# A hybrid decoder layer on one Trainium2 core: convolution taps taken from PSUM, the decays of a token block made in one go, and the decay product moved to GpSimd

## The chip, the core and the metric

The kernel runs as one program on one core of a Trainium2 chip. The metric is the device time of a run in microseconds; lower is better. The core has five engines with in-order queues of their own: TensorE (PE, with its weight loads shown as PEld), VectorE (DVE), ScalarE (ACT), GpSimd (POOL) and SyncE (SP), which issues all DMAs of this kernel. An engine that comes to an instruction whose inputs or buffers are not ready waits there, and everything behind it in its queue waits too.

## What is computed

One layer (DEPTH is 1) of a decoder on 2048 tokens of width 1024, all in float32: a mixer with three head groups, a SwiGLU block of width 2816, a gated per-layer embedding, and a final norm. What matters here are the mixer's group A (Mamba-2 SSD) and the depthwise convolutions of width 4, cut from the reference:

```
def _causal_dwconv(x, w, b):              # y[t] = b + sum_j w[j] * x[t - 3 + j], each channel alone
...
xbc = jax.nn.silu(_causal_dwconv(xbc, ssd_conv_w, ssd_conv_b))      # 896 channels: x 384, B 256, C 256
...
acs = jnp.cumsum(ac, axis=2)                                         # inside a chunk of 128 tokens
seg = acs[:, :, :, None, :] - acs[:, :, None, :, :]
lmat = jnp.exp(jnp.where(causal[None, None, :, :, None], seg, -jnp.inf))
scores = jnp.einsum("bclhn,bcshn->bclsh", cc, bc) * lmat             # (C B) times the decays
y_diag = jnp.einsum("bclsh,bcshp->bclhp", scores, xc)
decay_s = jnp.exp(acs[:, :, -1:, :] - acs)
states = jnp.einsum("bclhn,bclh,bclhp->bchpn", bc, decay_s, xc)
chunk_decay = jnp.exp(acs[:, :, -1, :])
...
xl = _causal_dwconv(lru_x, lru_conv_w, lru_conv_b)                   # group B, 256 channels
```

Group A has 6 heads of 64 in two groups with a state of 128; there are 16 chunks.

## The kernel before

Features lie on the 128 partitions, tokens along the free axis, in four blocks (`tb`) of 512 tokens. There are three stages. `phase1` norms the input, makes group B with its two convolution blocks per token block (`lru`), the values and gates, and q. `phase1b` makes group A: for each token block the normed input is loaded again and split, then come 7 calls of `conv` (one for each 128 channels of x, B and C), 4 calls of `ssd_chunk`, the z gate, k, and a norm whose result goes to DRAM. From the second block on, the attention of the first query block is interleaved with its matmuls (`Side`, `attention`), and in the last block the output projection of the first token block. `phase3` does the rest of the layer, with the other query blocks' attention interleaved.

Every large projection is `mm3`: input and weight are split in a rounded part and a rest, and three products of them are summed, so 24 matmuls of 128x512 per 128 output channels. Its weights come by `weight`: a DMA into `wst` (2 buffers), a rounding copy on ACT (L179), and the rest by a subtraction on POOL (L180), into `w` (3 buffers). The result lies in a PSUM bank `mm`, of which there are three. Single banks `xa` to `xe` serve the rest.

In `conv`, ACT copies the projection from `mm` to SBUF behind three columns of the block before (`raw`, one buffer, L435; L434 and L438 move the halo on DVE), then makes the last tap with the bias (L437), which is the last reader of the bank; the other three taps are multiply-adds on DVE (L440) of `raw` and the accumulator. For the 28 calls in `phase1b` a tanh (L444) and a product (L445) follow.

In `ssd_chunk`, bank `xb` holds in turn C B for two groups and B transposed (`pgb`), the diagonal product (`psd`, L509) and the transposed output (`py`); the row sums `ab` come by a DMA that broadcasts 6 rows over the partitions (L457, two buffers); L471 to L476 make the small decays; L479 makes, head by head, the differences with the mask added; ACT takes the exponential (L480); L488 multiplies it with C B from PSUM; `psd` takes it as the stationary operand.

The program is traced in the order of the code, with some parts at a higher priority, and a planner with a timing model of the engines then sets the order on each engine.

Of the kernel before, what the change touches and what calls it, by code (L numbers as in the profile page):

```python
# [13 lines left out]
ACT = mybir.ActivationFunctionType  # L14
ALU = mybir.AluOpType
# [4 lines left out]
P = 128  # L20
# [44 lines left out]
class Trunk:  # L65
# [317 lines left out]
    def phase1b(self, ctx):  # L383

        nc, tc, a = self.nc, self.tc, self.a
        pool = lambda name, bufs, **kw: ctx.enter_context(tc.tile_pool(name=name, bufs=bufs, **kw))
        one = pool("m2one", 1)
        two = pool("m2two", 2)
        self.load_mpar(one)
        hcw = self.t(one, [P, 35], "hcw")  # L390
        nc.vector.tensor_scalar(hcw, self.pc("scw", 0, 35), 0.5, None, op0=ALU.mult)
        self.neg = self.t(one, [P, P], "neg")
        nc.sync.dma_start(self.neg, a["cst"][:, 2])
        halo = self.t(one, [P, 7, 3], "halo")
        nc.gpsimd.memset(halo, 0.0)
        state = None
        for tb in range(NTB):
            if tb == 1:
                self.att_setup()
                self.side.start(self.attention(0, one, ("xc", "xd"), "xe"))  # L400
            u = []
            for k in range(KD):
                u.append(self.parts(k, self.load(self.du[tb, k]), nc.gpsimd))
            dtc = self.t(two, [P, 2, NCH, 6], "dtc")
            nc.sync.dma_start(dtc, self.ddt[tb])
            xbc = []
            for b in range(7):
                xbc.append(self.conv(a["w_xbc"][b], u, halo[:, b], hcw[:, 4 * b:4 * b + 4], hcw[:, 28 + b:29 + b],
                                     two, (two, f"xbc{b}", 1) if tb % 2 and b else (self.hp, "h", None), True))
            ys = [self.t(two, [P, TB], f"ys{j}", bufs=1) for j in range(3)]  # L410
            if tb == NTB - 1:

                yx = self.load_y(0)
            for c in range(NCH):
                state = self.ssd_chunk(tb, c, xbc, dtc, state, ys, two)
            if tb == NTB - 1:
                h = [self.mix(0, c, yx) for c in range(KD)]
                self.first = h, self.norm_split(h, "g2", eng=nc.vector, tag="xd")
            for b in range(3):
                ps = self.mm3(self.weight(a["w_z"][b], KD), u, 3)  # L420
                z = self.t(two, [P, TB], "t0")
                nc.scalar.activation(z, ps, ACT.Tanh, scale=0.5)
                nc.vector.scalar_tensor_tensor(z, z, 1.0, ps, op0=ALU.add, op1=ALU.mult)
                nc.vector.scalar_tensor_tensor(ys[b], ys[b], 0.5, z, op0=ALU.mult, op1=ALU.mult)
            for b in range(3):
                self.qk("w_k", b, tb, u, two)
            self.norm_store(ys, 384, 0, tb, "xa")

    def conv(self, wsrc, u, halo, cw, cb, two, dst, silu):

        nc = self.nc
        ps = self.mm3(self.weight(wsrc, KD), u, 3)
        raw = self.t(two, [P, TB + 3], "raw", bufs=1)
        nc.vector.tensor_copy(raw[:, 0:3], halo)  # L434
        nc.scalar.activation(raw[:, 3:], ps, ACT.Copy)  # L435
        acc = self.t(dst[0], [P, TB], dst[1], bufs=dst[2])
        nc.scalar.activation(acc, ps, ACT.Identity, bias=cb, scale=cw[:, 3:4])  # L437
        nc.vector.tensor_copy(halo, raw[:, TB:TB + 3])  # L438
        for j in range(3):
            nc.vector.scalar_tensor_tensor(acc, raw[:, j:j + TB], cw[:, j:j + 1], acc, op0=ALU.mult, op1=ALU.add)  # L440
        if not silu:
            return acc
        th = self.t(two, [P, TB], "t0")
        nc.scalar.activation(th, acc, ACT.Tanh)  # L444
        nc.vector.scalar_tensor_tensor(acc, th, 1.0, acc, op0=ALU.add, op1=ALU.mult)  # L445
        return acc

    def ssd_chunk(self, tb, c, xbc, small, state, ys, two):
        nc = self.nc
        cs = slice(c * P, (c + 1) * P)  # L450
        xs, bm, cm = xbc[0:3], xbc[3:5], xbc[5:7]
        first = state is None
        dt = small[:, 0, c]
        acol = small[:, 1, c]

        ab = self.t(two, [P, 6, P], "ab")
        nc.sync.dma_start(ab, self.drow[tb, c * 12 + 6:c * 12 + 12].partition_broadcast(P))  # L457

        ptr = self.ps("xa", (P, 3, P))
        for j in range(3):  # L460
            nc.tensor.transpose(ptr[:, j], xs[j][:, cs], self.ident)
        pgb = self.ps("xb", (P, 4, P))
        for g in range(2):
            nc.tensor.matmul(pgb[:, g], lhsT=bm[g][:, cs], rhs=cm[g][:, cs], start=True, stop=True)
        for g in range(2):
            nc.tensor.transpose(pgb[:, 2 + g], bm[g][:, cs], self.ident)
        bt = self.t(two, [P, 2, P], "bt", bufs=1)
        nc.scalar.activation(bt, pgb[:, 2:4], ACT.Copy)

        ex = self.t(two, [P, 3, 6], "ex")  # L470
        nc.vector.tensor_copy(ex[:, 0], ab[:, :, P - 1])  # L471
        nc.vector.tensor_tensor(ex[:, 1], ab[:, :, P - 1], acol, op=ALU.subtract)
        nc.vector.tensor_copy(ex[:, 2], acol)
        nc.scalar.activation(ex, ex, ACT.Exp)
        dec = self.t(two, [P, 6], "dec")
        nc.vector.tensor_tensor(dec, ex[:, 1], dt, op=ALU.mult)  # L476
        seg = self.t(two, [P, 6, P], "seg", bufs=1)
        for h in range(6):
            nc.vector.scalar_tensor_tensor(seg[:, h], ab[:, h], acol[:, h:h + 1], self.neg, op0=ALU.subtract, op1=ALU.add)  # L479
        nc.scalar.activation(seg, seg, ACT.Exp)  # L480

        px = ptr.rearrange("p j (i e) -> p (j i) e", i=2)
        xc = self.t(two, [P, 6, 64], "xc", bufs=1)
        nc.vector.tensor_tensor(xc, px, dt.unsqueeze(2).to_broadcast([P, 6, 64]), op=ALU.mult)
        xd = self.t(two, [P, 6, 64], "xd", bufs=1)
        nc.vector.tensor_tensor(xd, px, dec.unsqueeze(2).to_broadcast([P, 6, 64]), op=ALU.mult)
        for g in range(2):
            nc.vector.tensor_tensor(seg[:, 3 * g:3 * g + 3], seg[:, 3 * g:3 * g + 3],  # L488
                                    pgb[:, g].unsqueeze(1).to_broadcast([P, 3, P]), op=ALU.mult)

        yt = self.t(two, [P, 6, 64], "yt", bufs=1)
        if not first:
            pso = self.ps("xa", (P, 6, 64))
            for g in range(2):
                nc.tensor.matmul(pso[:, 3 * g:3 * g + 3], lhsT=cm[g][:, cs], rhs=state[:, 3 * g:3 * g + 3], start=True, stop=True)
            nc.vector.tensor_tensor(yt, pso, ex[:, 2].unsqueeze(2).to_broadcast([P, 6, 64]), op=ALU.mult)

        pst = self.ps("xa", (P, 6, 64))
        for g in range(2):
            nc.tensor.matmul(pst[:, 3 * g:3 * g + 3], lhsT=bt[:, g], rhs=xd[:, 3 * g:3 * g + 3], start=True, stop=True)  # L500
        ns = self.t(two, [P, 6, 64], "state")
        if first:
# [297 lines left out]

# [10 lines left out]
```

## Time and profile before

| | |
|---|---|
| median of 3 runs | 2930.53 us (2925.57 to 2932.34) |
| the profiled execution | 2928.33 us, of which span 2926.6 us |
| PE busy | 2812.5 us (96%) |
| DVE busy | 1751.9 us (60%) |
| ACT busy | 1175.7 us (40%) |
| POOL busy | 1213.2 us (41%) |
| mean granted clock of PE | 0.984 |

The span runs from the first to the last instruction; what lies around it is 1.7 us. Busy time of an engine includes time in which a started instruction is held up. `phase1` takes the first 325 us or so, `phase1b` the time to about 780 us, `phase3` the rest; neighbouring stages overlap a little.

### The profile page before, as it was taken

To read this page: it belongs to the slowest core of one execution; us is meant where nothing else is said; L and a number is where in the kernel's file an instruction comes from. 1 tells how busy PE (TensorE), PEld (TensorE's weight loads), DVE (VectorE), ACT (ScalarE), POOL (GpSimd) and SP (SyncE) were. 2 spreads that over 40 slices of the span, in tenths; PEclk is the share of its full clock that TensorE was granted. 3 is DMA by queue.
4 is the path that set the end of the run, shared out by engine and by line. 5 is a ranking of instruction groups with operands and counts; after the bars stand their busy time and mean duration, and the time that the engine had idled before them with its cause. 6 is when DMAs were issued, how large, how long until landed. Compare 5 with 4: busy or idle time off the path is not lost.

```text
span 2926.6 us, 35034 instructions
## 1 busy us (share of the span) xinstructions
PE 2812.5 (96%) x12981; PEld 2317.3 (79%) x12981; DVE 1751.9 (60%) x3001; ACT 1175.7 (40%) x1751; POOL 1213.2 (41%) x635
## 2 busy tenths in 40 slices
PE   6998999998999999999999999999999999999997
PEld 5777777777888888887888888788888887888885
DVE  7888768988754543637655446464665464523246
ACT  5555434444333332434444334344444343322233
POOL 5544445432443434443333334443333344444442
PEclk9999999998999999999999999999999999999998
DMA  5544544452354343434343334243443233332231
GB/s 181 172 164 159 162 142 141 132 162 80 136 157 131 119 122 104 142 123 133 118 147 104 127 105 146 100 146 115 133 122 114 91 130 108 116 97 92 100 100 65
DMA packets 156221, 368.60 MB, mean 126 GB/s; under 512 B 17644, under 2 KB 49036, under 8 KB 154508
## 3 DMA queue, kind: packets, MB, share of 16 engines
q1 hardware_dynamic: 156050, 366.36, 38.6%
q8 instruction: 103, 1.69, 0.2%
q14 instruction: 68, 0.56, 0.1%
HBM read 322.01 MB, written 44.29 MB: 125 GB/s over the span
## 4 chain that ended last, share of the span: by engine, by line
PE 72%; DVE 3%; issue 1%; DMA 1%; ACT 1%; POOL 0%; POOLq 0%; DVEq 0%; ACTq 0%
PE mm L191 20%; PE mm L192 20%; PE mm L190 20%; PE xd L609 2%; PE xd L608 2%; PE xa L603 1%; DMA ld<-dy 1%; PE xe L603 1%; PE xb L603 1%; PE xc L603 1%; PE xa L572 0%; PE xa L573 0%; DVE th L719 0%; DVE u L168 0%; PE xb L573 0%
## 5 line engine op out<-in xcount | busy, mean ns | idle before, releaser
L180 POOL TENSOR_TENSOR w<-wst,w 128x1024 fp32r<-128x1024 f32 (+1 forms) x424 | 1031.8, 2435 | 1365.6 <-ACT w L179 1300.5
L190 PE MATMUL mm<-u,w 128*128 128x512 f32 x3264 | 1295.9, 399 | 16.5 <-ACT u L200 8.9
L191 PE MATMUL mm<-u,w 128*128 128x512 f32 x3264 | 1289.6, 396 | 13.5 <-DVE u L201 13.5
L192 PE MATMUL mm<-u,w 128*128 128x512 f32 x3264 | 1289.9, 396 | 0.5 <-POOL w L180 0.5
L190 PEld LDWEIGHTS mm<-u,w 128*128 128x128 f32 x3264 | 619.1, 190 | 144.3 <-ACT u L200 10.8
L191 PEld LDWEIGHTS mm<-u,w 128*128 128x128 f32 x3264 | 619.0, 190 | 140.9 <-DVE u L201 17.9
L192 PEld LDWEIGHTS mm<-u,w 128*128 128x128 f32 x3264 | 618.6, 190 | 128.3 <-POOL w L180 0.9
L179 ACT ACTIVATE w<-wst 128x1024 fp32r<-128x1024 f32 (+1 forms) x424 | 440.5, 1040 | 525.1 <-PE mm L192 383.1
L685 DVE SCALAR_TENSOR_TENSOR u<-th,u 128x512 fp32r<-128x512 f32 x88 | 190.6, 2166 | 62.8 <-ACT u L684 62.7
L584 ACT ACTIVATE lg<-lg,m 128x128 f32<-128x128 f32 (+7 forms) x96 | 115.5, 1203 | 155.9 <-DVE m L582 150.9
L161 DVE TENSOR_TENSOR ssq<-ssq,sq 128x512 f32<-128x512 f32 x111 | 134.6, 1212 | 58.0 <-ACT sq L157 55.8
L682 DVE TENSOR_TENSOR th<-th,mm 128x512 f32<-128x512 f32 x88 | 60.4, 686 | 168.0 <-PE mm L192 167.3
L691 DVE TENSOR_TENSOR h<-h,mm 128x512 f32<-128x512 f32 x96 | 65.6, 686 | 127.1 <-PE mm L192 126.7
L680 ACT ACTIVATE th<-mm 128x512 f32<-128x512 f32 x88 | 52.6, 597 | 214.0 <-PE mm L192 213.7
L681 DVE SCALAR_TENSOR_TENSOR th<-th,mm 128x512 f32<-128x512 f32 x88 | 60.3, 685 | 113.1 <-ACT th L680 112.9
L564 POOL TENSOR_TENSOR cd<-cum,maskT 128x128 f32<-128x128 f32 x96 | 47.9, 499 | 182.3 <-DVE mx L577 92.3
L719 DVE SCALAR_TENSOR_TENSOR th<-th,lg 128x512 f32<-128x512 f32 x32 | 31.0, 968 | 111.5 <-ACT th L718 111.4
L587 DVE TENSOR_SCALAR lg<-lg,r 128x128 f32<-128x128 f32 (+7 forms) x96 | 93.6, 975 | 2.6
L609 PE MATMUL xd<-ph,vc 128*128 128x512 f32 x216 | 83.5, 390 | 0.0
L608 PE MATMUL xd<-ph,vc 128*128 128x512 f32 x216 | 80.8, 374 | 0.0
L607 DVE TENSOR_TENSOR ph<-xc,ph 128x512 fp32r<-128x512 f32 (+1 forms) x66 | 36.7, 556 | 48.4 <-ACT ph L606 48.4
L139 POOL TENSOR_TENSOR rr<-rv,mhalf 128x4 f32<-128x4 f32 x28 | 29.1, 1041 | 88.1 <-DVE rv L137 75.3
(293 smaller groups left out, 3212.2 us busy)
## 6 DMA issues: line engine op xcount, KB each, us to landing
wst<-in_w_gate SPq DMA_DIRECT2D x88, 512.0 KB, 3.5
wst<-in_w_up SPq DMA_DIRECT2D x88, 512.0 KB, 3.5
wst<-in_w_down SPq DMA_DIRECT2D x64, 448.0 KB, 3.3
wst<-in_w_out SPq DMA_DIRECT2D x32, 512.0 KB, 3.5
wst<-in_w_down SPq DMA_DIRECT2D x32, 512.0 KB, 3.5
wst<-in_w_pg SPq DMA_DIRECT2D x32, 512.0 KB, 3.5
vc<-dv SPq DMA_DIRECT2D x60, 256.0 KB, 3.8
wst<-in_w_xbc SPq DMA_DIRECT2D x28, 512.0 KB, 4.5
```

What stands on the lines that cost most here:

```text
L161: (eng or nc.gpsimd).tensor_tensor(acc, acc, s, op=ALU.add)
L179: nc.scalar.activation(w[:, 0], st, ACT.Copy)
L180: nc.gpsimd.tensor_tensor(w[:, 1], st, w[:, 0].bitcast(F32), op=ALU.subtract)
L190: nc.tensor.matmul(ps, lhsT=w[:, 0, k], rhs=x[:, 0], start=k == 0, stop=False)
L191: nc.tensor.matmul(ps, lhsT=w[:, 0, k], rhs=x[:, 1], start=False, stop=False)
L192: nc.tensor.matmul(ps, lhsT=w[:, 1, k], rhs=x[:, 0], start=False, stop=k == n - 1)
L584: nc.scalar.activation(lg, lg, ACT.Exp, bias=m, scale=1.0, accum_out=l)
L587: nc.vector.tensor_scalar(lg, lg, r, None, op0=ALU.mult)
L603: nc.tensor.transpose(pt[:, qi * P:(qi + 1) * P], probs[qi][:, kt * P:(kt + 1) * P], self.ident)
L608: nc.tensor.matmul(po[:, sl], lhsT=vc[:, kt], rhs=ph[:, 0, sl], start=kt == 0, stop=False)
L609: nc.tensor.matmul(po[:, sl], lhsT=vc[:, kt], rhs=ph[:, 1, sl], start=False, stop=kt == nkt - 1)
L685: nc.vector.scalar_tensor_tensor(hh[:, 1], th, 0.5, hh[:, 0].bitcast(F32), op0=ALU.mult, op1=ALU.subtract)
```

## The change

- `conv`: `raw` goes. The three taps read the bank `mm`, shifted by 1 to 3 columns in the accumulator. A copy of the last three columns (`end`, ACT) goes to POOL, where five small instructions make the next block's three halo sums; DVE adds the sums of the block before to the accumulator's first three columns.
- `decays` (new) issues, at the head of a token block, the four broadcasts into one `ab` of four chunks (one buffer) and makes the small decays of all four chunks with four DVE instructions and one exponential.
- `ssd_chunk`: DVE multiplies C B with a 0/1 triangle (`cb`); the differences are clipped at zero instead of masked, with one tensor operand instead of two; the product of the exponential and `cb` is made on POOL.
- A scratch area for dynamic DMAs is made smaller, which leaves more SBUF.

```diff
+        self.tri = self.t(one, [P, P], "tri")
+        nc.sync.dma_start(self.tri, a["cst"][:, 1])
...
-            dtc = self.t(two, [P, 2, NCH, 6], "dtc")
-            nc.sync.dma_start(dtc, self.ddt[tb])
+            small = self.decays(tb, two)
...
         ps = self.mm3(self.weight(wsrc, KD), u, 3)
-        raw = self.t(two, [P, TB + 3], "raw", bufs=1)
-        nc.vector.tensor_copy(raw[:, 0:3], halo)
-        nc.scalar.activation(raw[:, 3:], ps, ACT.Copy)
         acc = self.t(dst[0], [P, TB], dst[1], bufs=dst[2])
         nc.scalar.activation(acc, ps, ACT.Identity, bias=cb, scale=cw[:, 3:4])
-        nc.vector.tensor_copy(halo, raw[:, TB:TB + 3])
+        end = self.t(two, [P, 3], "end")
+        nc.scalar.activation(end, ps[:, TB - 3:], ACT.Copy)
         for j in range(3):
-            nc.vector.scalar_tensor_tensor(acc, raw[:, j:j + TB], cw[:, j:j + 1], acc, op0=ALU.mult, op1=ALU.add)
+            s = 3 - j
+            nc.vector.scalar_tensor_tensor(acc[:, s:], ps[:, :TB - s], cw[:, j:j + 1], acc[:, s:], op0=ALU.mult, op1=ALU.add)
+
+        nc.vector.tensor_tensor(acc[:, 0:3], acc[:, 0:3], halo, op=ALU.add)
+        nc.gpsimd.tensor_scalar(halo, end, cw[:, 0:1], None, op0=ALU.mult)
+        part = self.t(two, [P, 3], "part")
+        for j in (1, 2):
+            nc.gpsimd.tensor_scalar(part[:, j:], end[:, j:], cw[:, j:j + 1], None, op0=ALU.mult)
+            nc.gpsimd.tensor_tensor(halo[:, :3 - j], halo[:, :3 - j], part[:, j:], op=ALU.add)
...
+    def decays(self, tb, two):
+        nc = self.nc
+        dtc = self.t(two, [P, 2, NCH, 6], "dtc")
+        nc.sync.dma_start(dtc, self.ddt[tb])
+        ab = self.t(two, [P, NCH, 6, P], "ab", bufs=1)
+        for c in range(NCH):
+            nc.sync.dma_start(ab[:, c], self.drow[tb, c * 12 + 6:c * 12 + 12].partition_broadcast(P))
+        ex = self.t(two, [P, 3, NCH, 6], "ex")
+        nc.vector.tensor_copy(ex[:, 0], ab[:, :, :, P - 1])
+        nc.vector.tensor_tensor(ex[:, 1], ex[:, 0], dtc[:, 1], op=ALU.subtract)
+        nc.vector.tensor_copy(ex[:, 2], dtc[:, 1])
+        nc.scalar.activation(ex, ex, ACT.Exp)
+        nc.vector.tensor_tensor(ex[:, 1], ex[:, 1], dtc[:, 0], op=ALU.mult)
+        return dtc, ab, ex
...
-        ab = self.t(two, [P, 6, P], "ab")
-        nc.sync.dma_start(ab, self.drow[tb, c * 12 + 6:c * 12 + 12].partition_broadcast(P))
...
-        ex = self.t(two, [P, 3, 6], "ex")
-        nc.vector.tensor_copy(ex[:, 0], ab[:, :, P - 1])
-        nc.vector.tensor_tensor(ex[:, 1], ab[:, :, P - 1], acol, op=ALU.subtract)
-        nc.vector.tensor_copy(ex[:, 2], acol)
-        nc.scalar.activation(ex, ex, ACT.Exp)
-        dec = self.t(two, [P, 6], "dec")
-        nc.vector.tensor_tensor(dec, ex[:, 1], dt, op=ALU.mult)
+        cb = self.t(two, [P, 2, P], "cb", bufs=1)
+        nc.vector.tensor_tensor(cb, pgb[:, 0:2], self.tri.unsqueeze(1).to_broadcast([P, 2, P]), op=ALU.mult)
         seg = self.t(two, [P, 6, P], "seg", bufs=1)
         for h in range(6):
-            nc.vector.scalar_tensor_tensor(seg[:, h], ab[:, h], acol[:, h:h + 1], self.neg, op0=ALU.subtract, op1=ALU.add)
+            nc.vector.tensor_scalar(seg[:, h], ab[:, h], acol[:, h:h + 1], 0.0, op0=ALU.subtract, op1=ALU.min)
         nc.scalar.activation(seg, seg, ACT.Exp)
...
         for g in range(2):
-            nc.vector.tensor_tensor(seg[:, 3 * g:3 * g + 3], seg[:, 3 * g:3 * g + 3],
-                                    pgb[:, g].unsqueeze(1).to_broadcast([P, 3, P]), op=ALU.mult)
+            nc.gpsimd.tensor_tensor(seg[:, 3 * g:3 * g + 3], seg[:, 3 * g:3 * g + 3],
+                                    cb[:, g].unsqueeze(1).to_broadcast([P, 3, P]), op=ALU.mult)
...
-    nc = bacc.Bacc("TRN2", target_bir_lowering=False, num_devices=1)
+    nc = bacc.Bacc("TRN2", target_bir_lowering=False, num_devices=1, dynamic_dma_scratch_size=1024)
```

## Rows read from the trace of the kernel before

**Rows 1.** Busy us of each engine by stretch, TensorE's granted clock, DMA share, GB/s.
```profile
core 0: us, PE busy (x) PEld busy (x) DVE busy (x) ACT busy (x) POOL busy (x), PEclk, DMA share, GB/s
...
50.00:325.00 275.00, 250.50 (x1122) 209.04 (x1123) 236.06 (x338) 137.60 (x220) 136.63 (x74) 0.96 0.45 157
325.00:425.00 100.00, 88.22 (x395) 71.39 (x394) 68.49 (x129) 40.17 (x62) 48.39 (x26) 0.95 0.47 153
425.00:725.00 300.00, 275.04 (x1341) 224.45 (x1340) 264.86 (x596) 132.50 (x247) 121.68 (x81) 0.95 0.41 130
725.00:780.00 55.00, 55.00 (x283) 46.63 (x283) 37.96 (x66) 18.25 (x26) 24.35 (x12) 1.00 0.39 135
```

**Rows 2.** TensorE's waits, 325 to 425 us: total us, times, longest.
```profile
PE xb L464 <- DVE h L445: 4.7, 1, 4.7
PE mm L190 <- ACT h L437: 3.7, 5, 1.9
```

**Rows 3.** TensorE's waits, 425 to 725 us.
```profile
PE xa L149 <- DVE sq L147: 4.9, 4, 2.8
PE xe L609 <- DVE ph L607: 3.4, 3, 1.4
```

**Rows 4.** DVE in order of time, 655 to 690 us: start us, us, instruction.
```profile
657.95 4.34 DVE L440 SCALAR_TENSOR_TENSOR xbc<-raw,hcw,xbc 128x512 f32<-128x512 f32 x3 [0.50 <-ACT xbc L437]
...
670.69 2.41 DVE L587 TENSOR_SCALAR lg<-lg,r 128x128 f32<-128x128 f32 x1
```

**Rows 5.** POOL in order of time, 655 to 695 us.
```profile
658.95 2.80 POOL L180 TENSOR_TENSOR w<-wst,w 128x1024 fp32r<-128x1024 f32 x1 [6.57 <-ACT w L179]
...
669.98 3.04 POOL L180 TENSOR_TENSOR w<-wst,w 128x1024 fp32r<-128x1024 f32 x1 [0.47 <-ACT w L179]
```

**Rows 6.** DVE by form, 325 to 780 us: count, busy us, mean ns, idle before.
```profile
L440 DVE SCALAR_TENSOR_TENSOR h<-raw,hcw,h 128x512 f32<-128x512 f32 x48 | 55.5, 1156 | 3.4 <-ACT h L437 2.9
L440 DVE SCALAR_TENSOR_TENSOR xbc<-raw,hcw,xbc 128x512 f32<-128x512 f32 x36 | 40.4, 1121 | 1.4 <-ACT xbc L437 1.0
L479 DVE SCALAR_TENSOR_TENSOR seg<-ab,dtc,neg 128x128 f32<-128x128 f32 x96 | 39.6, 475 | 1.0 <-PE xb L509 1.0
...
L488 DVE TENSOR_TENSOR seg<-seg,xb 128x384 f32<-128x384 f32 x32 | 16.2, 544 | 2.2 <-ACT bt L468 2.2
...
L434 DVE COPY raw<-halo 128x3 f32<-128x3 f32 x28 | 9.5, 338 | 0.3
...
L476 DVE TENSOR_TENSOR dec<-ex,dtc 128x6 f32<-128x6 f32 x16 | 8.2, 510 | 2.7 <-ACT ex L474 2.5
L438 DVE COPY halo<-raw 128x3 f32<-128x3 f32 x28 | 8.1, 291 | 5.1 <-ACT raw L435 4.7
...
L473 DVE COPY ex<-dtc 128x6 f32<-128x6 f32 x16 | 4.8, 298 | 0.0
...
L587 DVE TENSOR_SCALAR lg<-lg,r 128x256 f32<-128x256 f32 x6 | 2.1, 355 | 0.1
```

**Rows 7.** DVE by form, 0 to 325 us.
```profile
L440 DVE SCALAR_TENSOR_TENSOR lx<-raw,mpar,lx 128x512 f32<-128x512 f32 x24 | 32.2, 1341 | 1.5 <-ACT lx L437 1.0
...
L211 DVE SCALAR_TENSOR_TENSOR x<-x,par,xc 128x512 f32<-128x512 f32 x32 | 21.3, 739 | 0.6 <-PE xc L149 0.6
```

**Rows 8.** POOL by form, 325 to 780 us.
```profile
L180 POOL TENSOR_TENSOR w<-wst,w 128x1024 fp32r<-128x1024 f32 x55 | 138.8, 2524 | 146.6 <-ACT w L179 134.2 <-PE mm L192 4.6 <-PE xa L495 3.7
...
L505 POOL TENSOR_TENSOR state<-state,ex 128x384 f32<-128x384 f32 x15 | 13.9, 924 | 37.6 <-DVE state L506 33.1 <-DVE raw L434 3.6 <-DVE rl L143 0.9
L564 POOL TENSOR_TENSOR cd<-cum,maskT 128x128 f32<-128x128 f32 x24 | 12.0, 499 | 42.2 <-DVE mx L577 19.3 <-DMA cum<-dcum 12.9 <-DMA ab<-drow 5.8
...
L395 POOL MEMSET halo<- 128x21 f32 x1 | 0.1, 111 | 0.0
```

**Rows 9.** The decay product and its reader on TensorE, 425 to 445 us.
```profile
426.54 1.01 DVE L488 TENSOR_TENSOR seg<-seg,xb 128x384 f32<-128x384 f32 x2
...
427.69 1.52 PE L509 MATMUL xb<-xc,seg 128*128 128x64 f32 x12
```

**Rows 10.** SyncE's own waits, 300 to 780 us.
```profile
SPq L457 <- DVE seg L479: 15.3, 4, 5.8
```

More of the change, by code (lines that the diff above doesn't have):

```diff
@@ L414, in phase1b @@
             for c in range(NCH):
-                state = self.ssd_chunk(tb, c, xbc, dtc, state, ys, two)
+                state = self.ssd_chunk(c, xbc, small, state, ys, two)
             if tb == NTB - 1:
@@ L446, in conv, with ssd_chunk @@
         return acc
-    def ssd_chunk(self, tb, c, xbc, small, state, ys, two):
+    def decays(self, tb, two):
[12 more added lines that the diff above has]
+        return dtc, ab, ex
+    def ssd_chunk(self, c, xbc, small, state, ys, two):
         nc = self.nc
@@ L452, in ssd_chunk @@
         first = state is None
-        dt = small[:, 0, c]
-        acol = small[:, 1, c]
-        ab = self.t(two, [P, 6, P], "ab")
-        nc.sync.dma_start(ab, self.drow[tb, c * 12 + 6:c * 12 + 12].partition_broadcast(P))
+        dtc, ab, ex = small
+        dt, acol, ab = dtc[:, 0, c], dtc[:, 1, c], ab[:, c]
+        whole, dec, since = ex[:, 0, c], ex[:, 1, c], ex[:, 2, c]
         ptr = self.ps("xa", (P, 3, P))
@@ L495, in ssd_chunk @@
                 nc.tensor.matmul(pso[:, 3 * g:3 * g + 3], lhsT=cm[g][:, cs], rhs=state[:, 3 * g:3 * g + 3], start=True, stop=True)
-            nc.vector.tensor_tensor(yt, pso, ex[:, 2].unsqueeze(2).to_broadcast([P, 6, 64]), op=ALU.mult)
+            nc.vector.tensor_tensor(yt, pso, since.unsqueeze(2).to_broadcast([P, 6, 64]), op=ALU.mult)
         pst = self.ps("xa", (P, 6, 64))
@@ L504, in ssd_chunk @@
         else:
-            nc.gpsimd.tensor_tensor(ns, state, ex[:, 0].unsqueeze(2).to_broadcast([P, 6, 64]), op=ALU.mult)
+            nc.gpsimd.tensor_tensor(ns, state, whole.unsqueeze(2).to_broadcast([P, 6, 64]), op=ALU.mult)
             nc.vector.tensor_tensor(ns, ns, pst, op=ALU.add)
```

## The prediction

> **What bounds the kernel now.** TensorE sets the end, so I asked first where it loses time, and took the busy time of each engine by stage. In the 300 us from 425 to 725 TensorE stands still for 25.0 us while DVE is busy for 264.9 of 300 (88%); from 725 to 780, in the same stage, DVE is at 69% and TensorE does not stop at all [rows 1]. From 325 to 425 TensorE stands still for another 11.8 us. [...] Together 57 us are lost in `phase1b`. In `phase1`, from 50 us on, it is 24.5 us of standstill and 4% of 275 us, 11 us: 35 us. That bounds what this change can win, since it touches no line of `phase3`.
>
> Then TensorE's own waits. Nearly all name DVE, or ACT behind DVE: the ring of projection banks (L190 waits for the last ACT reader L437, 3.7 us), the first chunk for the last silu (4.7 us) [rows 2], the norms and attention's probabilities [rows 3]. In the second list there are thirteen entries of 24.2 us in all; I count 9.9 us of them to attention and 7.6 us to the norms' chains.
>
> Last, why DVE is so full. Its timeline has ordinary instructions that suddenly take over 2 us: three taps of 4.34 us in all, and a 128x128 scaling of 2.41 us [rows 4]. Each meets the start of a weight subtraction on POOL, at 658.95 and 669.98 us, and ends about when that does [rows 5]. In the lists by form, instructions with both tensors in SBUF have inflated means (taps 1156, 1121 and 1341 ns), while those with one tensor in PSUM are steady (L211 at 739 ns, the same operation and width; L488 at 544) [rows 6, 7].
>
> [...]
>
> **The change, part by part (`phase1b`, DVE first).**
> - Taps: 84 instructions of 55.5 + 40.4 = 95.9 us [rows 6] become 84 x 0.739 = 62.1 us by L211 [rows 7]: 33.8 us less. Bounds: nothing, if the hold-up just passes to the next two-SBUF instruction, and 33.8.
> - Halo: the two copies (9.5 + 8.1 us) go; 28 additions on three columns come, each between 0.30 and 0.51 us by the tiny L473 and L476 [rows 6], 8 to 14 us; with 11 the saving is 6.6.
> - Small decays: 64 tiny instructions become 16; 48 x 0.30 to 0.51 is 14 to 24 us; I take 18, since the other two forms lie between.
> - Differences: 96 x 0.475 us now. A scaling with one tensor and twice the width has 0.355 [rows 6], so the saving is 0 to 11.5 us; as that one too can be held up, 5.
> - Product: 16.2 us go; `cb`, two thirds as wide as L488 and also from PSUM, is at most 16 x 0.544 = 8.7 us, by width 6: 10 less.
>
> That is 73 us. Against it stands new work on POOL that can hold DVE up: 32 products of about 0.92 us by L505 (30 us), and 28 x 5 tiny instructions, each between the memset's 0.11 and L564's 0.50 us [rows 8]; at 0.25 that is 35 us. POOL goes from 194 to 259 of 455 us. I charge DVE 10 us (bounds 0 and the 30 us of the products) and keep 63. Three of four token blocks lie in the 300 us stretch: 47 of 264.9 us, DVE at 73% there, near the 69% at which TensorE does not stop [rows 1].
>
> [...]
>
> What leaves ACT is a copy of 512 columns for one of three. The exponential, transposes and matmuls stay. Ring: the last reader of a bank is now the third tap instead of L437. Before, though, ACT's copy of the next projection waited for these same taps (`raw` has one buffer), so the bank came free behind DVE already. I take no new loss, and keep as a loss the case that DVE runs late: L190 is then what waits.
>
> DMAs: the same 16 broadcasts, four at a time at the head of a block. With one buffer the group waits for the last difference of the block before, on SP, ahead of that block's weight loads. SP waits there today, 15.3 us in four times, the longest 5.8 [rows 10]. TensorE has two split weights ahead, so I cost it at nothing; behind a wait longer than these two projections the weights would be late next. Load of the triangle, scratch size: nothing; all DMAs are issued by SP.
>
> The halo work on POOL waits for `end`, that is for the projection just made; the weight subtractions behind it on POOL are for projections two further on. Nothing, unless POOL fills.
>
> The product on POOL is on the path to L509. Today DVE ends it 0.14 us before L509 starts in one chunk [rows 9], so it can be tight. The two products take 1.85 instead of 1.01 us, and a weight subtraction of 2.5 us may stand in front. Bounds per chunk: 0 if the planner has other matmuls in between, and 0.84 + 2.5 = 3.3 us. I take 0.5 us, as POOL idles more than four tenths of the time: 16 x 0.5 = 8 us.
>
> **The sum.** Of the 36.8 us of standstill in `phase1b` I count 7.6 to norm chains, which are dependent steps, and some 26 to DVE's queue. With DVE near 70% I let 70% of the queue's and 30% of the chains' go: 18 + 2 = 20 us. The clock's 20 us follow in proportion: 20 x 20/36.8 = 11. In `phase1` the taps lose 24 x (1.341 - 0.739) = 14.4 us and the copies about 5 more, 8% of DVE's 236 us; 8% of 35 is 3 us. Less 8 for POOL: 20 + 11 + 3 - 8 = 26 us. From 2928.3 (span 2926.6 and 1.7 around it) that gives 2902 us. The median of the three runs lies 2.2 us above the profiled execution, which is within their spread, so I leave the number.
>
> **The rivals.**
> 1. *Forecast: DVE's queue shortens and TensorE waits less.* 2902 us. With 13 us of standstill and 7 of clock back and POOL at 14 the gain is 9 (2919); with 30 and 16 back and POOL at 1 it is 48 (2880). Chance 0.60.
> 2. *Nearly all of it comes back.* DVE below the level at which TensorE stops, and no standstill means no low clock: 57 + 10 from `phase1` and nothing for POOL, 2861 us; down to 48 us, where case 1 ends, 2880. The stretch from 725 us speaks for it, the norm chains against it. Chance 0.14.
> 3. *POOL becomes what L509 waits for.* The product stands behind weight subtractions of 2.5 us in POOL's in-order queue, `xb` stays taken, and the whole chunk moves. The 34 us of gain are used up at 34/16 = 2.1 us per chunk. At the bound of 3.3 us it is 53 us, and as much of it again as the clock takes by its present ratio (20/36.8), 29: 82 - 34 = 48 us slower, 2976; at 2.7 us 33 slower, 2961, and at 2.4 us about 2950. For it: POOL in-order, one `seg`, one `xb`. Against it: its idle share, and that what L505 waits for is mostly DVE [rows 8]. Chance 0.12.
>    [...]
> 4. *The stalls are chains, not a queue.* Each wait is for an instruction whose own inputs came late (silu after the last tap, norm sums), or the hold-ups pass from the taps to other two-SBUF instructions. Then the gain is 5 us at the most, and POOL's 8 us eat it: 2923 to 2934. Chance 0.14.
>
> **How the numbers follow.** Changes under 0.2% (5.9 us) are about what a measurement of this kernel cannot tell from none. Cases 1 and 2 are faster: 0.74; case 4 the same: 0.14; case 3 slower: 0.12. The likeliest time is 2902, its own range 2880 to 2920. Leaving out the lower end of case 2 and most of case 3 gives 2866 to 2938.
>
> **What the profile after would show.** Taps at 0.73 to 0.76 us without outliers; DVE in the stretch of the last three blocks near 73%; TensorE's idle time in `phase1b` about halved, its clock there at 0.97 or more; L190 hardly waiting; waits for POOL's product of some 8 us. Wrong would make it: a list headed by L509 waiting for POOL (case 3), means of other two-SBUF instructions grown by what the taps lost (case 4), SP late with weights, or L190 waiting for the taps.

## The result, and the profile after

The changed kernel takes **2904.1 us** (median of 4 runs, 2901.8 to 2905.94) against 2931.44 (2925.57 to 2933.14) of the kernel before in runs taken beside it: a ratio of **0.991, 95% interval 0.9893 to 0.9927**. Forecast were 2902. The profiled span fell from 2926.6 to 2902.2 us, by 24.4.

To see where, I cut the span at two instructions that both kernels have: ACT's first last-tap instruction of `phase1b` (L437 before, L435 after, writing `h`) and the first tanh of `phase3`. `phase1` ends at 326.8 instead of 331.5 us (4.7 less), `phase1b` takes 458.6 instead of 483.4 (24.8 less), and `phase3`, which the change does not touch, takes 2116.8 instead of 2111.7 (5.1 more).

Busy time by stretch after the change, in the columns of [rows 1]:

```profile
50.00:325.00 275.00, 249.38 (x1128) 208.06 (x1127) 222.80 (x329) 137.16 (x223) 141.95 (x112) 0.96 0.46 161
325.00:425.00 100.00, 91.53 (x440) 76.31 (x439) 69.61 (x124) 39.06 (x64) 69.65 (x78) 0.98 0.50 156
425.00:725.00 300.00, 286.08 (x1443) 239.53 (x1443) 235.18 (x555) 127.85 (x245) 180.35 (x205) 0.97 0.44 141
725.00:780.00 55.00, 55.00 (x264) 46.10 (x263) 34.43 (x49) 20.26 (x29) 26.21 (x14) 1.00 0.37 127
```

From 425 to 725 us TensorE's standstill fell from 25.0 to 13.9 us and its granted clock rose from 0.95 to 0.97; DVE went from 264.9 to 235.2 us busy, POOL from 121.7 to 180.4.

DVE by form, 325 to 785 us; these lines answer to [rows 6]:

```profile
L496 DVE TENSOR_SCALAR seg<-ab,dtc 128x128 f32<-128x128 f32 x96 | 36.4, 446 | 1.1 <-PE xb L526 1.1
...
L440 DVE SCALAR_TENSOR_TENSOR h<-mm,hcw,h 128x510 f32<-128x510 f32 x16 | 11.9, 747 | 0.4
L440 DVE SCALAR_TENSOR_TENSOR h<-mm,hcw,h 128x511 f32<-128x511 f32 x16 | 11.9, 745 | 0.2
...
L440 DVE SCALAR_TENSOR_TENSOR xbc<-mm,hcw,xbc 128x511 f32<-128x511 f32 x12 | 8.9, 742 | 0.2
...
L442 DVE TENSOR_TENSOR h<-h,halo 128x3 f32<-128x3 f32 x16 | 8.4, 524 | 0.3
...
L442 DVE TENSOR_TENSOR xbc<-xbc,halo 128x3 f32<-128x3 f32 x12 | 7.3, 606 | 0.1
L493 DVE TENSOR_TENSOR cb<-xb,tri 128x256 f32<-128x256 f32 x16 | 6.7, 418 | 8.8 <-ACT bt L490 8.6
```

All forms of the tap now have a mean of 742 to 747 ns; before they had 1156 and 1121. The shortest, middle and longest of `h`, first before and then after (ns), show that only the long ones went:

```profile
L440 DVE SCALAR_TENSOR_TENSOR h<-raw,hcw,h x48: 736/752/2952, 332.7 to 637.9; 128x512 f32<-128x512 f32 x48
```

```profile
L440 DVE SCALAR_TENSOR_TENSOR h<-mm,hcw,h x48: 729/748/751, 328.2 to 612.9; 128x509 f32<-128x509 f32 x16, 128x510 f32<-128x510 f32 x16, 128x511 f32<-128x511 f32 x16
```

The new additions on three columns are the opposite: 524 and 606 ns for so little work. One place in time, on DVE and then on POOL (start us, us, instruction), shows both:

```profile
657.76 2.32 DVE L440 SCALAR_TENSOR_TENSOR xbc<-mm,hcw,xbc 128x509 f32<-128x509 f32 x3 [0.81 <-ACT end L437]
660.11 1.05 DVE L442 TENSOR_TENSOR xbc<-xbc,halo 128x3 f32<-128x3 f32 x1
```

```profile
658.75 2.40 POOL L180 TENSOR_TENSOR w<-wst,w 128x1024 fp32r<-128x1024 f32 x1 [0.63 <-ACT w L179]
```

Three taps with one input in PSUM pass beside the weight subtraction in 2.32 us; in [rows 4, 5] three taps with both inputs in SBUF took 4.34 beside one. The halo addition behind them, both inputs in SBUF, ends only when the subtraction does, at 661.15 us.

TensorE's waits, from 325 to 425 us and then from 425 to 725 (total us, times, longest), which answer to [rows 2, 3]:

```profile
PE mm L190 <- DVE h L440: 4.4, 1, 4.4
PE xa L512 <- DVE xd L503: 4.0, 2, 2.4
```

```profile
PE mm L190 <- DVE h L669: 2.1, 1, 2.1
PE xa L483 <- DVE sq L222: 2.0, 1, 2.0
PE xb L486 <- DVE xbc L452: 2.0, 1, 2.0
...
PE mm L190 <- DVE ex L466: 1.1, 1, 1.1
...
PE xb L526 <- DVE xc L501: 0.7, 1, 0.7
```

L526 is the reader of POOL's product (L509 before). It waits for DVE's `xc` once, and for POOL nowhere in the stage.

### The profile page after: what moved, and what is told of

The parts are those of the page before. It is cut to its first block, busy times and chain, and to the rows that moved or that the text cites. A ratio compares the mean times of both kernels' runs of the same rounds, so it can differ in the third digit from the quotient of the medians.

```text
span 2902.2 us, 35105 instructions
## 1 busy us (share of the span) xinstructions
PE 2801.0 (97%) x12981; PEld 2315.4 (80%) x12981; DVE 1680.8 (58%) x2901; ACT 1156.4 (40%) x1739; POOL 1287.6 (44%) x847
## 4 chain that ended last, share of the span: by engine, by line
PE 80%; DVE 10%; DMA 3%; issue 3%; ACT 2%; POOL 1%; SPq 0%; POOLq 0%; DVEq 0%; ACTq 0%
PE mm L191 23%; PE mm L192 23%; PE mm L190 23%; PE xd L626 2%; PE xd L625 2%; DVE u L201 1%; POOL w L180 1%; DMA ld<-dy 1%; PE xa L620 1%; PE xe L620 1%; DVE seg L496 1%; PE xc L620 1%; ACT w L179 1%; PE xb L620 1%; DVE t L367 1%
## 5 line engine op out<-in xcount | busy, mean ns | idle before, releaser
L180 POOL TENSOR_TENSOR w<-wst,w 128x1024 fp32r<-128x1024 f32 (+1 forms) x424 | 1020.5, 2408 | 1252.3 <-ACT w L179 1201.8
L190 PE MATMUL mm<-u,w 128*128 128x512 f32 x3264 | 1294.6, 398 | 21.4 <-ACT u L200 8.9
L190 PEld LDWEIGHTS mm<-u,w 128*128 128x128 f32 x3264 | 618.3, 190 | 148.9 <-ACT u L200 10.8
L624 DVE TENSOR_TENSOR ph<-xc,ph 128x512 fp32r<-128x512 f32 (+1 forms) x66 | 36.7, 556 | 49.5 <-ACT ph L623 49.5
```

What stands on the lines that cost most here:

```text
L180: nc.gpsimd.tensor_tensor(w[:, 1], st, w[:, 0].bitcast(F32), op=ALU.subtract)
L190: nc.tensor.matmul(ps, lhsT=w[:, 0, k], rhs=x[:, 0], start=k == 0, stop=False)
```

## The experiments

The kernels were measured in three groups, each beside runs of the kernel before (medians 2930.65 us from `conv_only` to `product_dve`, 2931.2 from `pool_reads` to `halo_act`, 2931.95 for the rest); the ratio is against these. Stage is `phase1b` between the two cuts. "Idle" is TensorE's standstill in it, "clock" the stage times one minus the mean granted clock. "Held" is a sum of my own over the trace: for each DVE instruction of the stage, its duration beyond the least of its line and form, where that is over 0.1 us. DVE's and POOL's busy times are those of the instructions that start and end in the stage. Sizes in us.

| kernel | median | ratio, 95% interval | stage | idle | clock | held | DVE busy | POOL busy |
|---|---|---|---|---|---|---|---|---|
| before | 2931 | 1 | 483.4 | 36.7 | 18.8 | 97.8 | 391.8 | 204.0 |
| after | 2904.1 | 0.991 [0.9893, 0.9927] | 458.6 | 22.4 | 11.9 | 66.2 | 340.3 | 276.8 |
| conv_only | 2898.13 | 0.9887 [0.9874, 0.9901] | 457.3 | 19.2 | 13.7 | 64.9 | 356.1 | 243.9 |
| ssd_only | 2933.02 | 1.0007 [0.9998, 1.0016] | 483.8 | 40.9 | 23.9 | 111.3 | 386.2 | 240.8 |
| taps_from_copy | 2931.27 | 1.0001 [0.9992, 1.001] | 484.1 | 33.4 | 22.2 | 98.3 | 370.8 | 299.1 |
| product_dve | 2900.88 | 0.9898 [0.9884, 0.9911] | 459.4 | 20.3 | 13.7 | 62.8 | 349.9 | 254.8 |
| pool_reads | 2931.62 | 1.0003 [0.9995, 1.0012] | 491.2 | 47.0 | 25.6 | 95.3 | 385.0 | 296.7 |
| pool_writes | 2888.83 | 0.9859 [0.9846, 0.9873] | 447.2 | 14.6 | 10.2 | 75.4 | 360.6 | 289.0 |
| dve_load | 2901.14 | 0.99 [0.9885, 0.9915] | 462.7 | 24.4 | 18.8 | 71.0 | 371.7 | 243.6 |
| halo_act | 2917.73 | 0.9957 [0.9945, 0.997] | 472.9 | 30.6 | 18.8 | 61.9 | 350.1 | 194.7 |
| before_writes | 2927.94 | 0.9987 [0.9978, 0.9996] | 484.3 | 36.1 | 23.9 | 108.4 | 394.4 | 257.6 |
| after_writes | 2925.58 | 0.9982 [0.9973, 0.9991] | 478.7 | 36.3 | 20.5 | 80.2 | 344.4 | 320.3 |
| conv_halo_dve | 2914.98 | 0.9945 [0.9933, 0.9957] | 474.0 | 29.6 | 22.2 | 81.4 | 389.6 | 196.9 |
| conv_decays | 2895.02 | 0.9876 [0.9861, 0.9891] | 454.0 | 16.3 | 13.7 | 55.1 | 342.7 | 248.0 |

**The two halves of the change.** `conv_only` is the kernel before with the new `conv`; `ssd_only` the changed kernel with the old one:

```diff
@@ conv_only, against before (ssd_only: the reverse, against after)
-        nc.scalar.activation(raw[:, 3:], ps, ACT.Copy)
...
-            nc.vector.scalar_tensor_tensor(acc, raw[:, j:j + TB], cw[:, j:j + 1], acc, op0=ALU.mult, op1=ALU.add)
+            s = 3 - j
+            nc.vector.scalar_tensor_tensor(acc[:, s:], ps[:, :TB - s], cw[:, j:j + 1], acc[:, s:], op0=ALU.mult, op1=ALU.add)
...
```

> The kernel before with the new conv alone (taps from PSUM, halo sums on POOL); the SSD chunk as before. Theory (DVE's queue): DVE loses 34 us of taps and 7 of copies in the second stage, a little over half of the 73 us, and POOL gets no product, so some 16 to 20 us of the 27 come: ratio 0.993 to 0.995. Rival (chains: the gain comes from the chunk's shorter steps): under 6 us, 0.998 or more. If the conv is all that matters, 0.991 or less.

> The changed kernel with the old conv (raw copy in one buffer, taps from SBUF, halo copies on DVE). Theory: DVE loses 33 us, but the products on POOL hold up taps that still need both inputs from SBUF, so only 5 to 10 us of the 27 come: ratio 0.9966 to 0.998. Rival (POOL's product is harmful by itself): slower than before, above 1.000. The taps' mean should stay above 1100 ns.

Measured 2898.13 and 2933.02 us. The convolution alone brings everything; the SSD half alone nothing that can be measured. Two DVE lines of `ssd_only`, 325 to 785 us, say where that half's DVE savings went:

```profile
L441 DVE SCALAR_TENSOR_TENSOR h<-raw,hcw,h 128x512 f32<-128x512 f32 x48 | 57.0, 1187 | 2.8 <-ACT h L438 2.0
...
L439 DVE COPY halo<-raw 128x3 f32<-128x3 f32 x28 | 16.0, 573 | 4.3 <-ACT raw L436 4.2
L435 DVE COPY raw<-halo 128x3 f32<-128x3 f32 x28 | 13.1, 467 | 0.6
```

The unchanged copies of the halo take 16.0 and 13.1 us where they took 8.1 and 9.5, the taps 57.0 for 55.5 [rows 6]: beside POOL's product the held time rises from 97.8 to 111.3 us, and DVE's busy time falls by 5.6 only.

**The same kernel, its taps from SBUF.** `taps_from_copy` adds a copy on ACT and lets the taps read it; everything else stays as in the changed kernel.

```diff
+        raw = self.t(two, [P, TB], "raw")
+        nc.scalar.activation(raw, ps, ACT.Copy)
...
-            nc.vector.scalar_tensor_tensor(acc[:, s:], ps[:, :TB - s], cw[:, j:j + 1], acc[:, s:], op0=ALU.mult, op1=ALU.add)
+            nc.vector.scalar_tensor_tensor(acc[:, s:], raw[:, :TB - s], cw[:, j:j + 1], acc[:, s:], op0=ALU.mult, op1=ALU.add)
```

> The changed kernel, with the projection copied to SBUF by ACT once more (two buffers) and the taps reading that copy; everything else as changed. If the taps' gain is that they need no SBUF input beside the accumulator, their mean goes from 745 back to over 1050 ns and 15 to 20 us of the 27 go: 2917 to 2924. If the gain is that the one buffer of raw no longer ties the ACT copy to the taps before, this kernel keeps it: 2901 to 2908.

Measured 2931.27 us: all of the gain is gone, more than the 15 to 20 us expected. Its taps by form on DVE, 325 to 785 us:

```profile
L442 DVE SCALAR_TENSOR_TENSOR h<-raw,hcw,h 128x511 f32<-128x511 f32 x16 | 16.6, 1038 | 0.2
L442 DVE SCALAR_TENSOR_TENSOR xbc<-raw,hcw,xbc 128x511 f32<-128x511 f32 x12 | 16.1, 1339 | 0.1
...
L442 DVE SCALAR_TENSOR_TENSOR h<-raw,hcw,h 128x509 f32<-128x509 f32 x16 | 13.6, 853 | 4.5 <-ACT h L437 4.5
```

and 425 to 725 us of `taps_from_copy`, then of `conv_only`, in the columns of [rows 1]:

```profile
425.00:725.00 300.00, 276.04 (x1341) 227.44 (x1340) 245.21 (x533) 129.81 (x254) 183.43 (x207) 0.94 0.42 132
```

```profile
425.00:725.00 300.00, 289.89 (x1475) 243.11 (x1475) 248.80 (x611) 133.04 (x257) 159.38 (x185) 0.98 0.44 141
```

DVE is busy for 245 us in the one and 249 in the other, and TensorE stands still for 24 and 10. So the total of DVE's busy time does not decide; single instructions that last too long, and so end too late, go with the loss. Here the copy has two buffers and the third tap no longer holds the bank, so neither explains the old loss. The added copy also makes each convolution's chain longer; this run does not separate that from the source of the taps, since no kernel keeps the copy and reads the bank.

**Where the product is made.** `product_dve` has `nc.vector` for `nc.gpsimd` in the product with `cb`.

```diff
-            nc.gpsimd.tensor_tensor(seg[:, 3 * g:3 * g + 3], seg[:, 3 * g:3 * g + 3],
+            nc.vector.tensor_tensor(seg[:, 3 * g:3 * g + 3], seg[:, 3 * g:3 * g + 3],
```

> The changed kernel with the product of the exponential and C B on DVE instead of POOL (same operands). DVE gets 32 times about 0.55 us, 18 us, which can be held up by weight subtractions, POOL loses 33 us. By my charge of 8 us for POOL's product on the path, against 18 us of DVE work of which a third to a half would show: 2900 to 2908, the same within what can be told. If the product on POOL was costly: 2896 or less. If taking it off DVE was a main part of the gain: 2912 or more.

Measured 2900.88 us, 3 less than after, with overlapping intervals. Moving the product to POOL takes 23.9 us of DVE instructions away and lowers DVE's busy time by 9.6 (349.9 to 340.3); it does not shorten the kernel.

**POOL's reading, apart from POOL's load.** Three kernels are `conv_only` with dummy work per convolution of `phase1b` (on a tile that nothing else uses, no part of the layer): an addition on POOL, two fills on POOL, or a fill on DVE. They also have the changed kernel's smaller scratch area, which `conv_only` has not. Nothing waits for the dummies, and the planner put them early: POOL's run from about the start of the stage to 477 us, DVE's to 391.

```diff
+        nc.gpsimd.tensor_tensor(self.dum, self.dum, self.dum, op=ALU.add)      # pool_reads
...
+        for _ in range(2):                                                     # pool_writes
+            nc.gpsimd.memset(self.dum, 0.0)
...
+        nc.vector.memset(self.dum, 0.0)                                        # dve_load
```

> conv_only with one more POOL instruction in each of the second stage's 28 convolutions: a 128x1024 addition that reads SBUF and belongs to nothing (about 2.4 us each, 67 us in all). Theory formed on the first four runs: what TensorE loses in the second stage goes with the time for which POOL holds DVE instructions up (98 us held and 56 lost before, 65 and 33 in conv_only), not with DVE's total. POOL's reading time grows by a quarter, so some 18 us more are held and about 12 us lost: 2906 to 2920 against conv_only's 2898. Rival (POOL only costs where its own results are late): these have no reader, so 2895 to 2902.

> conv_only with two POOL fills of 128x1024 per convolution instead (about 1.05 us each by the fill of 128x512 at 0.52, 59 us in all): POOL is as busy as in pool_reads but reads nothing from SBUF. If the hold-up needs a POOL instruction that reads SBUF: 2895 to 2902, as conv_only. If any busy POOL holds DVE up or delays its queue: as pool_reads, 2906 or more.

> conv_only with one DVE fill of 128x1024 per convolution of the second stage: 28 times 0.5 to 1.1 us, 15 to 30 us of DVE work, about what the SSD part saves, without SBUF input and without reader. Theory (hold-ups, not load): 2895 to 2903, as conv_only. Rival (my prediction's own step: DVE's load sets TensorE's waits, and the SSD part loses its gain elsewhere): 10 us more, 2906 to 2912.

Measured 2931.62, 2888.83 and 2901.14 us. The dummies on POOL, 325 to 800 us, and all engines from 425 to 725, first of `pool_reads`, then of `pool_writes`:

```profile
L451 POOL TENSOR_TENSOR dum<-dum 128x1024 f32<-128x1024 f32 x28 | 54.2, 1937 | 0.2
...
425.00:725.00 300.00, 274.10 (x1380) 229.53 (x1379) 256.21 (x591) 128.72 (x254) 174.68 (x200) 0.95 0.44 138
```

```profile
L452 POOL MEMSET dum<- 128x1024 f32 x56 | 53.5, 956 | 0.7
...
425.00:725.00 300.00, 292.40 (x1504) 246.44 (x1503) 257.07 (x616) 134.14 (x258) 175.70 (x206) 0.98 0.46 143
```

POOL's dummy time is the same, 54.2 and 53.5 us, and so are DVE's and POOL's busy times in the stretch. TensorE stands still for 25.9 us in it with additions and 7.6 with fills. The loss lies where the dummies run; these are 325 to 475 us of the two:

```profile
325.00:475.00 150.00, 113.45 (x489) 92.00 (x488) 106.21 (x171) 47.38 (x81) 120.71 (x105) 0.85 0.37 118
```

```profile
325.00:475.00 150.00, 141.91 (x676) 117.76 (x675) 114.53 (x204) 60.74 (x102) 141.49 (x165) 0.98 0.46 144
```

TensorE stands still for 36.6 us of these 150 with additions, for 8.1 with fills and for 8.8 in `conv_only`; from 475 to 790 us it is 10.4, 6.5 and 10.4. The additions raise the held time of `conv_only` by 30 us (64.9 to 95.3), the fills by 10. So `pool_reads` comes out above the 2906 to 2920 us expected. TensorE's longest waits in it, 325 to 790 us, are for DVE again, the ring of banks first:

```profile
PE mm L190 <- DVE h L441: 11.3, 2, 6.1
PE mm L190 <- DVE ex L481: 7.3, 1, 7.3
```

In this pair the longer hold-up goes with the dummies that read SBUF: the 128x128 differences, two SBUF inputs, have 597 ns in `pool_reads` and 446 in `pool_writes`. Instruction by instruction it is plainer. Six differences beside an addition and then six beside fills (start us, us, instruction):

```profile
447.32 4.07 DVE L488 SCALAR_TENSOR_TENSOR seg<-ab,dtc,neg 128x128 f32<-128x128 f32 x6
447.99 1.89 POOL L451 TENSOR_TENSOR dum<-dum 128x1024 f32<-128x1024 f32 x1
```

```profile
383.64 1.81 DVE L489 SCALAR_TENSOR_TENSOR seg<-ab,dtc,neg 128x128 f32<-128x128 f32 x6
383.93 6.02 POOL L452 MEMSET dum<- 128x1024 f32 x6
```

Of the differences that begin at least 0.3 us before a dummy ends, the six beside additions take 1.25 to 1.98 us and end 0.15 us after the addition does, the fourteen beside fills take 0.34. The taps of `h`, from PSUM, have means of 740 to 742 ns by form in `pool_reads` and 741 to 759 in `pool_writes`.

In `dve_load`, 25.5 us of fills on DVE (28 of 0.91 us) cost 3 us; but all of them ran between 326 and 391 us, where DVE had room (48.8 of the 70 us from 325 to 395 in `conv_only`), so the run says nothing of more DVE work in the fuller blocks behind. That `pool_writes` is 9 us faster than `conv_only` I did not expect: each edit makes the planner lay out the whole program anew, and the fills, or the scratch area, may do that too.

**Fills in the other two kernels.** The same two fills (dummy work again) in the kernels before, there with the smaller scratch area, and after:

```diff
+        for _ in range(2):
+            nc.gpsimd.memset(self.dum, 0.0)
```

> The kernel before with the two POOL fills per convolution of pool_writes (no SBUF input, no reader). The fills change what the planner sees, so its order changes as it did there. If the 9 us that pool_writes won over conv_only were an effect of the order alone, this kernel lies within 8 us of before on either side: 2923 to 2939. If fills help by themselves (POOL's reads moved to better times): 2915 to 2922.

> The changed kernel with the same two POOL fills per convolution. Order alone: within 8 us of the changed kernel, 2896 to 2912. If fills help by themselves: 2893 or less. If POOL, with its products and now 83% busy or so in the second stage, becomes what the diagonal product waits for: 2915 or more.

Measured 2927.94 and 2925.58 us: 4 us less than before, but 21 more than after. So the gain in `pool_writes` does not come from fills as such, and the changed kernel loses with them where `conv_only` gains. In `after_writes` POOL is busy for 320 of 478.7 us; TensorE's first waits, 325 to 805 us, are

```profile
PE xa L516 <- DVE xd L507: 9.4, 3, 4.4
PE xa L149 <- DVE sq L147: 4.3, 3, 1.8
PE mm L190 <- DVE h L442: 4.1, 2, 3.9
```

None names the product. What makes DVE's `xd` late can be read from the order on DVE: the six differences stand right in front of it, and in the changed form, one tensor and a scalar, they are held up beside fills too (DVE, POOL, and DVE before the longest wait):

```profile
385.71 3.12 DVE L500 TENSOR_SCALAR seg<-ab,dtc 128x128 f32<-128x128 f32 x6
385.66 4.07 POOL L453 MEMSET dum<- 128x1024 f32 x4
```

```profile
410.87 5.21 DVE L500 TENSOR_SCALAR seg<-ab,dtc 128x128 f32<-128x128 f32 x6
416.46 0.54 DVE L507 TENSOR_TENSOR xd<-xa,ex 128x384 f32<-128x384 f32 x1
```

Those that begin beside a fill take 0.85 to 1.08 us with a least of 0.27, where the old form took 0.34. Six take 5.21 and 3.88 us before TensorE's two long waits for `xd`, 8.6 us together; in the changed kernel its 4.0 us at L512 stand behind such groups too, of 7.75 and 5.16 us. The difference is a part of the 21 us: from 675 to 725 us, long after the last fill at 504, TensorE loses 10.5 us for 3.9 in the changed kernel, and how much of that is the new order is not settled.

**Where the halo is made.** `conv_halo_dve` is `conv_only` with the five small instructions on DVE; in `halo_act` ACT seeds the accumulator's first three columns with the halo sums as bias and makes the next sums from PSUM.

```diff
-        nc.gpsimd.tensor_scalar(halo, end, cw[:, 0:1], None, op0=ALU.mult)
+        nc.vector.tensor_scalar(halo, end, cw[:, 0:1], None, op0=ALU.mult)     # and the other four: conv_halo_dve
...
+        for i in range(3):                                                     # halo_act
+            S(acc[:, i:i + 1], ps[:, i:i + 1], ACT.Identity, bias=halo[:, i:i + 1], scale=cw[:, 3:4])
...
+        for i, j, k in ((0, 1, 1), (1, 1, 2), (0, 2, 2)):
+            S(halo[:, i:i + 1], ps[:, e + k:e + k + 1], ACT.Identity, bias=halo[:, i:i + 1], scale=cw[:, j:j + 1])
```

> conv_only with the five small halo instructions on DVE instead of POOL: POOL loses 36 x 5 instructions that read SBUF (some 50 us in the second stage), DVE gets as many of 0.15 to 0.2 us (25 us), two of five with two SBUF inputs. If POOL's reading time is what costs: 2888 to 2896. If the new DVE instructions are held up as often as the halo additions (0.3 to 0.6 us each): 2898 to 2908.

> conv_only with the halo taken off POOL and DVE: ACT makes the three halo sums from PSUM and adds them as the bias of the first three columns (seven small and one large ACT instruction per convolution, no end copy). DVE loses its 28 exposed additions (9 us), POOL its 140 tiny instructions in the stage (some 50 us, most of them reading SBUF). Theory: 5 to 15 us fewer held, 3 to 10 us faster than conv_only: 2888 to 2895. Rival (ACT's longer chain before the taps keeps the bank taken): 2898 or more.

Measured 2914.98 and 2917.73 us, 17 and 20 more than `conv_only`, the first above both of its ranges, the second where its rival lay. On DVE the stage's busy time rises by 33.5 us and the held time by 16.5. On ACT the held time is low (61.9) and the loss is still high. Here ACT is 40 us busier from 325 to 800 us (236.1 for 196.3), and TensorE's longest waits are for the taps behind it (L444, 13.8 us); that ACT's lateness is the cause is argued, not tested. Three lines of it, with 48.3 us in instructions of one column:

```profile
L441 ACT ACTIVATE halo<-mm,halo,hcw 128x1 f32<-128x1 f32 x84 | 24.4, 360 | 0.4
L437 ACT ACTIVATE h<-mm,halo,hcw 128x1 f32<-128x1 f32 x48 | 13.7, 359 | 0.0
...
L437 ACT ACTIVATE xbc<-mm,halo,hcw 128x1 f32<-128x1 f32 x36 | 10.2, 351 | 0.0
```

**The convolution and the decays.** `conv_decays` is the changed kernel with the old masked differences and the old product on DVE, without `cb`.

```diff
-            nc.vector.tensor_scalar(seg[:, h], ab[:, h], acol[:, h:h + 1], 0.0, op0=ALU.subtract, op1=ALU.min)
+            nc.vector.scalar_tensor_tensor(seg[:, h], ab[:, h], acol[:, h:h + 1], self.neg, op0=ALU.subtract, op1=ALU.add)
...
-            nc.gpsimd.tensor_tensor(seg[:, 3 * g:3 * g + 3], seg[:, 3 * g:3 * g + 3],
-                                    cb[:, g].unsqueeze(1).to_broadcast([P, 3, P]), op=ALU.mult)
+            nc.vector.tensor_tensor(seg[:, 3 * g:3 * g + 3], seg[:, 3 * g:3 * g + 3],
+                                    pgb[:, g].unsqueeze(1).to_broadcast([P, 3, P]), op=ALU.mult)
```

> conv_only with the decays of a token block made in one go, and nothing else of the SSD part: masked differences and product on DVE from PSUM as before. DVE loses 48 tiny instructions (24.7 us by their rows in conv_only, 3.5 remain). If DVE's load hardly matters, as dve_load says: 2892 to 2902. If the one ab buffer and the wait for four broadcasts cost what the instructions save: 2898 to 2908. If the tiny instructions were worth their share of DVE's time: 2888 or less.

Measured 2895.02 us, 0.9876 [0.9861, 0.9891]: the fastest without dummy work, 9 us below after, with the least held time of all (55.1). Against `conv_only` it is 3 us, with overlapping intervals.

## Why the prediction was right, and which steps were not

**The total and its place.** Case 1 came: 2904.1 for 2902. The stage terms came out too: `phase1b` gave 24.8 us for a forecast 23 (20 + 11 - 8), `phase1` 4.7 for 3. In `phase1b` idle and clock together fell from 55.5 to 34.3 us, 21 for the forecast 31; the other 3.6 us of the 24.8 lie outside these two sums. The 20 us of the clock, which the 57 us count in beside 25.0 and 11.8 of standstill, are 5% of 400 us by the 0.95 of [rows 1]; in the trace of before the granted clock stands at 1.00 or at 0.50, and the table has 18.8 us for it, 11.9 after: 6.9 came back for the 11 taken in proportion. The 8 us charged for waits at POOL's product are not in the list: L526 never waits for POOL. So 31 and 8 were each too large, and that their difference came near is luck. In case 3, the 2.1 us per chunk leave out the clock's share that the sums behind it count in; with it the gain would be used up at 1.4 us.

**The mechanism of the taps** holds. They were priced at 739 ns and have 742 to 747; 95.9 us became 62.5, 33.4 less for 33.8. The bound of nothing, for a hold-up that passes to the next instruction, did not come: of the held time before, 33.7 us lay on the taps and 64.1 on the rest of DVE; after, none and 66.2. All four kernels whose taps read SBUF lie at 2928 to 2933 us; of the ten whose taps read PSUM, six lie at 2889 to 2904, and the other four have work added or moved. `pool_reads` beside `pool_writes` shows for the differences, with two SBUF inputs, that it is POOL's reading that costs, not POOL being busy (597 ns for 446, with 54.2 and 53.5 us of dummies). Why an operand in PSUM frees an instruction, no run here shows.

**DVE's sum.** Forecast 73 less by parts and 10 back. By parts it was 68: taps 33.4, halo 1.9 (17.6 for 15.7, not 6.6: the additions have 524 and 606 ns where I took 0.39), decays 20.4 (23.9 for 3.5), differences 3.2, product 9.5. Busy time fell by 51.5 (391.8 to 340.3), so some 17 came back for the 10 charged. DVE from 425 to 725 us is at 78%, not 73.

**The step that failed** is the one that turned DVE's total into TensorE's gain: "With DVE near 70% I let 70% of the queue's and 30% of the chains' go", with the taps, decays, differences and product all counting alike by their microseconds. They don't. `ssd_only` took the SSD half's savings and gained nothing; `taps_from_copy` has DVE busy for 21 us less in the stage than before and gains nothing; `conv_only` leaves DVE 16 us busier than after and is not slower. So the total was near for another reason than the sum gave: the convolution brought all of it, where the expectation for `conv_only` still had 16 to 20 of the 27 us. More work on DVE is not free either: `conv_halo_dve`, which adds it in all four blocks, loses 17 us to `conv_only` with DVE busy for 33.5 us more, 16.5 of them held. What TensorE's loss goes with more closely is the held time: 95 to 111 us in the five kernels that gain 4 us at the most (before among them), 55 to 71 in five of the six fastest. It is not a law: `pool_writes` has 75.4 and the least loss, `halo_act` 61.9 and a large one through ACT. The SSD half frees DVE of 33 us by its rows and puts 32.9 us of reading products on POOL; on its own it raises the held time by 13.5, and on top of the convolution by 1.3.

POOL's new rows, 325 to 780 us, answer to [rows 8]:

```profile
L505 POOL TENSOR_TENSOR seg<-seg,cb 128x384 f32<-128x384 f32 x32 | 32.9, 1049 | 30.5 <-DVE cb L493 16.5 <-DVE carry L548 7.7 <-DVE m L599 3.2
...
L446 POOL TENSOR_SCALAR part<-end,hcw 128x1 f32<-128x1 f32 x28 | 13.0, 464 | 2.5
```

The product took 1049 ns for 924, and POOL waits for DVE before it, not TensorE behind it. So rival 3 did not come, nor in `after_writes`, where POOL is busy for 320 us and TensorE still waits for no product.

**Ring.** "L190 hardly waiting" was wrong: from 325 to 425 us it waits 4.4 us for the taps (3.7 for L437 before), which the prediction had named as a sign of being wrong. "No new loss" holds within a microsecond: the wait changed its name.

**Broadcasts.** "Nothing" was about right for TensorE, but DVE pays, as the two waits after, DVE's and then SP's, show:

```profile
DVE ex L465 <- DMA ab<-drow: 9.9, 4, 3.7
```

```profile
SPq L463 <- DVE seg L496: 6.2, 3, 3.7
```

With one buffer `ab` is loaded late, and DVE stands 9.9 us at four block heads (0.8 before); SP's own wait fell from 15.3 to 6.2 us [rows 10]. TensorE's share in it is the 1.1 us at L466's line above.

**Left out of the forecast:** `phase3`'s 5.1 us. No line of it changed; among all these kernels it takes between 2111.1 and 2118.7 us. Its cause is open, as is why fills made `conv_only` faster. Dummy fills moved three kernels by 4, 9 and 21 us, and how much of that is a new order is not known; so the 6 us between after and `conv_only`, and the 3 between `conv_only` and `conv_decays`, are put to no edit. The rivals of much more gain (case 2) and of none (case 4) fell: of 34 us still lost in the stage, the norms' chains are part, as they were before.

## What to carry to other kernels

Where GpSimd works beside VectorE, compare the mean of each VectorE form with its least: what is inflated here takes all its tensors from SBUF (of the stage's instructions with a tensor in PSUM, 293 before and 361 after, none lasts 0.04 us longer than the least of its line and form), and one operand left in PSUM freed the taps (1156 and 1121 ns before, 742 to 747 after), even read three times. Price a move to GpSimd by what it will hold up, not only by what it takes off VectorE: here 32 products moved over bought nothing. And where a planner reorders the program at each edit, take differences of a few tenths of a percent as no evidence for the edit.

## Unexpected of the hardware

- An instruction with one tensor and a scalar is held up too, and beside POOL's fills as well: the differences with one tensor operand (L496) have a mean of 446 ns and a least of 272, and 545 with fills. Copies of 128x6 (`ex<-ab`) have 793 ns with additions, 784 with fills and 408 with neither.
- Small GpSimd work is dear: 199 to 464 ns for one or two columns (L446, L447), where I had taken 0.25 us; and ACT's instructions of one column from PSUM, with bias and scale by pointer, cost 0.35 to 0.36 us each.
- An addition on GpSimd with the same tile as both inputs took 1937 ns at 128x1024, the weight subtraction of two tiles 2458, a fill 956.
